# A hybrid decoder layer on one core: the input norm in fixed turns on each engine, idle products of another kind, and the keys' products tied

## The chip, the core and the metric

The kernel runs on one core of a Trainium2 chip. The time is device microseconds of one execution. Engines are called as in the profile: PE (TensorE, matrix products; PEld is its weight load), ACT (ScalarE), DVE (VectorE), POOL (GpSimd) and SP (SyncE, which here only issues transfers). Each engine works through its own list of instructions in order and waits on semaphores for what other engines or transfers deliver.

## What is computed

512 tokens of 1024 values go through one layer. The input is normed once, and everything else starts from the normed input `h`: the mLSTM branch, the sliding-window attention with its queries, keys and values, and two gates. The output projection, an MLP, a gated embedding and a last norm follow.

```python
def rmsnorm(x, g):
    xf = x.astype(jnp.float32)
    xf = xf * lax.rsqrt(jnp.mean(xf * xf, axis=-1, keepdims=True) + EPS)
    return xf.astype(x.dtype) * g.astype(x.dtype)
...
        h = rmsnorm(x, norm_mix_g[i])
        proj = h @ w_in[i]
        qk_ml, v_ml, o_ml, if_pre, q_sw, k_sw, v_sw, g_a, g_b = jnp.split(proj, split_idx, axis=-1)
```

The change concerns the norm, the product that gives `v_sw` (256 columns) and `if_pre` (8 columns), and where the product that gives `k_sw` may stand.

## The kernel before

Every float32 product is done as three products of two parts: an operand is split into a high part, a copy in the type fp32r, and a low part, the difference. `split` does the first on ACT and the second on DVE; `pairs` lists the three products (high with high, high with low, low with high), and `chain` issues them (L171). A product's last operand is thus always a low part.

The start works on four tiles of 128 tokens (`NT` = 4), in this order:

- SP loads the norm's weight (`grow`, one row of 1024), then x tile by tile (`xt`, the first in two halves) and the three pieces (`K3`: 3, 3 and 2 of the 8 blocks of 128 rows) of the weight of the values and gates (`w_vsif`, raw pieces `wv`, split into `wh` and `wl` by `load_vs_w`, the high part on POOL, L327, the low part on DVE, L328).
- The weight's row is split into parts (`gparts`) and spread over 128 partitions by four products with a row of ones, into `gmix` (L275). Between them PE does idle products of a matrix of ones (`stir`, L263): 5 before, 1 in the middle, 3 behind.
- `norm(m)`: ACT squares the tile and sums (L296), ACT takes the root (L283), DVE the reciprocal (L285), and DVE scales the tile by it and by `gmix` in two halves (L300).
- `columns(m, xn)`: PE transposes the eight blocks (L311, into two banks for even tiles, `pst`, and one wide one for odd tiles, `psa`), ACT copies the high part into `h` (L316), DVE makes the low part (L317), and ACT keeps an unsplit copy `hf` for tiles 1 to 3 (L321).
- The values' product of a tile is 24 products of 264 columns (`mm_tok`), 9, 9 and 6 by the weight's pieces; ACT copies out the values (`vs`, L352) and DVE adds the gates' bias (L353).
- Then come the keys, two groups of 24 products of 512 columns (`proj_T(w_ksw, i, ps_t)`), the first queries (`q_proj(0)`) and the mLSTM's values (`by_tokens`).

A scheduler sets the order of instructions within an engine from their order in the program, their readiness and the places given by `tc.issue_after` (what is inside comes behind the named instruction) and `tc.keep_in_program_order` (the instruction keeps its place among those of its engine). Before, only the idle products and the weight's four products are kept in order. A tile of memory comes from a pool with a few buffers under one tag; an instruction that takes a buffer over waits for those that used it. The raw weights (`wr`) have four, their parts (`wh`, `wl`) four each, the banks `pst`, `psg`, `psa` two each, the scratch of tokens (`lm`, which holds `grow`, the scaled tiles `xn` and later four of the mLSTM value weight's eight pieces `wq`) four.

Of the kernel before, what the change touches and what calls it, by code (L numbers as in the profile page):

```python
# [36 lines left out]
def block_kernel(  # L37
# [49 lines left out]
    def nm(s):  # L87
        n_names[0] += 1
        return f"{s}_{n_names[0]}"


    def ps_g():
        return pp.tile([P, 512], F32, tag="g", bufs=2, name=nm("psg"))

    def ps_t():
        return pp.tile([P, 512], F32, tag="t", bufs=2, name=nm("pst"))

    def ps_a():
        return pp.tile([P, 1024], F32, tag="a", bufs=2, name=nm("psa"))
# [34 lines left out]
    def split(dst, src, scale=None):  # L134

        if scale is None:
            A.copy(dst[0], src)  # L137
            last_low[0] = V.tensor_sub(dst[1], src, r32(dst[0]))  # L138
# [26 lines left out]
        return [(a[0], b[0]), (a[0], b[1]), (a[1], b[0])]  # L165

    last_mm = [None]

    def chain(ps, ops, first, last, parts=False):
        for i, (l, r) in enumerate(ops):  # L170
            last_mm[0] = T.matmul(ps, l, r, start=first and i == 0, stop=last and i == len(ops) - 1, skip_group_check=parts)  # L171

    def quads(src, tags):

# [17 lines left out]
    def mm_tok(ps, w, acts, m, first=True, last=True):  # L192
# [4 lines left out]
        chain(ps, ops, first, last)  # L197

    nc.scalar.preload_act_table_set("sqrt_and_others")


    ident = cp.tile([P, P], F32, name="ident")
# [29 lines left out]
            o = slice(c * D // n, (c + 1) * D // n)  # L232
            nc.sync.dma_start(out=xt[m][:, o], in_=x[m * P : (m + 1) * P, o])

    grow = tok_scratch("grow")[:1, :]
    nc.sync.dma_start(out=grow, in_=g_mix)
    load_x(0, 2)

    K3 = [slice(0, 3), slice(3, 6), slice(6, 8)]
# [18 lines left out]

    idle = [ps_g(), ps_g()]

    def stir(n, bank=0):
        for i in range(n):
            tc.keep_in_program_order(T.matmul(idle[bank][:, :P], ones, ones, start=True, stop=True))  # L263

    one_row = c1.tile([1, P], F32R, name="one_row")
    A.copy(one_row, ones[:1, :])
    gmix = ps_a()
    gparts = [[act_r("gm")[:1, :] for _ in range(2)] for _ in range(2)]
    for c in range(2):
        split(gparts[c], grow[:, c * 512 : (c + 1) * 512])  # L270
    stir(5)
    for i in range(2):
        for c in range(2):
            tc.keep_in_program_order(
                T.matmul(gmix[:, c * 512 : (c + 1) * 512], one_row, gparts[c][i], start=i == 0, stop=i == 1, skip_group_check=True)  # L275
            )
        stir(1 if i == 0 else 3, i)

    def rstd_of(ss, n):

        w = ss.shape[1]
        sd = small("sd", w)
        A.activation(sd, ss, AF.Sqrt, bias=eps_t, scale=1.0 / n)  # L283
        rs = small("rs", w, 5)
        V.reciprocal(rs, sd)  # L285
        return rs
# [3 lines left out]
    h2, hT = big_hl("h")  # L290
    hf = [None]

    def norm(m):
        xn = tok_scratch("xn")
        ss = small("ss", 1)
        A.activation(xn, xt[m], AF.Square, accum_out=ss)  # L296
        rs = rstd_of(ss, D)
        for c in range(2):
            o = slice(c * 512, (c + 1) * 512)
            done = V.scalar_tensor_tensor(xn[:, o], xt[m][:, o], rs, gmix[:, o], ALU.mult, ALU.mult)  # L300
        return xn, done.ins

    def columns(m, xn):

        if m % 2:
            ps = ps_a()
            halves = [ps[:, :512], ps[:, 512:]]
        else:
            halves = [ps_t(), ps_t()]
        for k in range(KT):  # L310
            T.transpose(halves[k // 4][:, k % 4 * P : (k % 4 + 1) * P], xn[:, k * P : (k + 1) * P], ident)  # L311
        n = 8 if m % 2 else 4
        for k in range(0, KT, n):
            dst = [t[:, k : k + n, m * P : (m + 1) * P] for t in h2]
            src = (ps if m % 2 else halves[k // 4]).rearrange("p (k c) -> p k c", k=n)
            first = A.copy(dst[0], src)  # L316
            second = V.tensor_sub(dst[1], src, r32(dst[0]))  # L317
            if m:
                if k == 0:
                    hf.append(tk("hf")[:, :D].rearrange("p (k c) -> p k c", k=KT))  # L320
                A.copy(hf[m][:, k : k + n, :], src)  # L321
        return first.ins, second.ins

    def load_vs_w(c):
        n = K3[c].stop - K3[c].start
        hl = [wp.tile([P, 1024], F32R, tag=t, bufs=WB, name=nm(t))[:, : n * 264] for t in ("wh", "wl")]
        G.tensor_copy(hl[0], wv[c][:, : n * 264])  # L327
        V.tensor_sub(hl[1], wv[c][:, : n * 264], r32(hl[0]))  # L328
        return [q.rearrange("p (k c) -> p k c", k=n) for q in hl]

    xn, normed = norm(0)
    with tc.issue_after(normed):
        wv[0] = load_vs_w(0)
    on_scalar, _ = columns(0, xn)
    with tc.issue_after(on_scalar):
        xn, normed = norm(1)
    with tc.issue_after(normed):
        wv[1:] = [load_vs_w(1), load_vs_w(2)]
    _, on_vector = columns(1, xn)
    for m in range(NT):  # L340
        if m == 1:
            with tc.issue_after(on_vector):
                xn, _ = norm(2)
            columns(2, xn)
        elif m == 2:
            columns(3, norm(3)[0])

        ps = ps_g()
        for c in range(3):
            mm_tok(ps[:, :264], wv[c], hT[K3[c]], m, first=c == 0, last=c == 2)  # L350
        t = sp.tile([P, 256], F32, tag="vs", bufs=4, name=nm("vs"))
        A.copy(t, ps[:, :256])  # L352
        gate_in = V.tensor_add(gt[:, m, :], ps[:, 256:264], bif)  # L353
# [8 lines left out]


    hf[0] = tk("hf")[:, :D].rearrange("p (k c) -> p k c", k=KT)
    with tc.issue_after(gate_in.ins):
        hi, lo = [r32(t[:, :, :P]) for t in h2]
        V.tensor_add(hf[0], hi, lo)

# [33 lines left out]
    HALF = [slice(0, 64), slice(64, 128)]  # L402
    kk, kl = [], []
    for i in range(2):
        ps = proj_T(w_ksw, i, ps_t)
        both = [act_r("kk"), act_r("kk")]
        low = [act_r("kl"), act_r("kl")]
        for ab in range(2):
            s, o = HALF[ab], HALF[1 - ab]
            A.copy(both[ab][s, :], ps[s, :])  # L410
            V.tensor_sub(low[ab][s, :], ps[s, :], r32(both[ab][s, :]))
            nc.sync.dma_start(out=r32(both[ab])[o, :], in_=r32(both[ab])[s, :])
            nc.sync.dma_start(out=r32(low[ab])[o, :], in_=r32(low[ab])[s, :])
        kk.append(both)
        kl.append(low)
# [12 lines left out]
    q_proj(0)  # L428

    S3, S4 = [], []  # L430

# [92 lines left out]

    pg = ps_a()
    pgi, pgf = pg[:, :512], pg[:, 512:]
    for m in range(NT):
        T.transpose(pgi[:4, m * P : (m + 1) * P], gt[:, m, :4], ident)
        T.transpose(pgf[:4, m * P : (m + 1) * P], gt[:, m, 4:], ident)
    by_tokens(w_vml, post_by_tokens(put_v), True)  # L530


    def row(n):
# [220 lines left out]
    V.tensor_scalar_mul(nsink, sink, -1.0)  # L754


    vd = [None] + [sp.tile([P, 256], F32, tag="vd", bufs=2, name=nm("vd")) for _ in range(2)] + [vs[3]]
    for n in (3, 2, 1):
        V.tensor_sub(vd[n], vs[n], vs[n - 1])
# [671 lines left out]
```

## Time and profile before

| | |
|---|---|
| Time, median of 3 runs | 882.57 us (881.98 to 882.72) |
| The profiled execution | 882.08 us, span 880.3 us |
| PE busy | 868.6 us, 99% of the span |
| DVE, ACT, POOL busy | 662.1, 481.8, 28.9 us |
| PE busy in 0 to 22 us | 19.80 us |
| PE busy in 22 to 100 us | 78.00 us |
| Granted TensorE clock | 0.999 |

A row of the timeline reads: start, duration, engine, line, operation, output <- inputs, partitions x elements, and how many instructions are merged into the row; in brackets the idle time of the engine before it and what ended it. Starts are counted from the span's start. Durations of products are modelled and overlap, so the distance between starts is the time that one takes from the next. A row of stretches gives: the stretch, its length, then the busy time of PE, PEld, DVE, ACT and POOL with their numbers of instructions, the granted clock, the share of the transfer engines and GB/s.

### The profile page before, as it was taken

Reading aid. Unit: us, or ns where it says so; the run is one execution under the profiler, and the core shown is the slowest. Engines: PE = TensorE matmul, PEld = TensorE weight load, DVE = VectorE, ACT = ScalarE, POOL = GpSimd, SP = SyncE. Lnnn points to the kernel's source line nnn. Section 1 sums busy time; section 2 is a strip of 40 time slices with the busy share of each in tenths; the row PEclk is TensorE's granted clock in tenths of the full one; section 3 lists DMA queues with packets and bytes.
Section 4 is the critical chain, followed back from the end, with each engine's and each line's share of the span. In section 5 each row is a group of like instructions: output and inputs, shape, how many; then the busy total and the mean of one; then the engine's idle time right before and its main releaser. Section 6 shows DMA issues by size and latency. Waiting matters only on the chain.

```text
span 880.3 us, 11620 instructions
## 1 busy us (share of the span) xinstructions
PE 868.6 (99%) x4404; PEld 727.8 (83%) x4404; DVE 662.1 (75%) x980; ACT 481.8 (55%) x808; POOL 28.9 (3%) x52
## 2 busy tenths in 40 slices
PE   8999999999999999999999999999999999999996
PEld 7888889998777777888888888888888888878886
DVE  6999888875789876666896669657956884689566
ACT  6684554544775768743344665356335534544843
POOL 1111010000000000000020000000000000000000
PEclk9999999999999999999999999999999999999999
DMA  7765244436122162364244612620452064101402
GB/s 266 211 180 184 73 156 163 170 110 193 49 73 72 49 211 75 100 241 139 72 90 149 220 44 77 210 96 1 140 171 72 1 195 140 48 25 54 163 1 95
DMA packets 32361, 105.16 MB, mean 119 GB/s; under 512 B 4525, under 2 KB 5037, under 8 KB 32306
## 3 DMA queue, kind: packets, MB, share of 16 engines
q1 hardware_dynamic: 28002, 93.15, 32.0%
q0 software_dynamic: 4160, 11.02, 4.8%
q8 instruction: 34, 0.56, 0.3%
q10 hardware_dynamic: 144, 0.26, 0.1%
q14 instruction: 21, 0.17, 0.1%
HBM read 91.30 MB, written 8.40 MB: 113 GB/s over the span
## 4 chain that ended last, share of the span: by engine, by line
PE 75%; DVE 3%; ACT 3%; issue 1%; DMA 0%; SPq 0%; ACTq 0%
PE psg L171 43%; PE psp L171 22%; PE psa L171 4%; PE psa L831 1%; PE pst L747 1%; DVE wl L138 1%; ACT lm L712 1%; PE psa L819 1%; ACT wh L137 1%; PE psa L689 1%; PE psa L690 1%; PE psa L726 0%; PE pst L873 0%; PE psp L988 0%; DVE qs L425 0%
## 5 line engine op out<-in xcount | busy, mean ns | idle before, releaser
L137 ACT CAST wh<-wr 128x1024 fp32r<-128x1024 f32 x138 | 144.8, 1051 | 179.0 <-PE psg L171 74.8
L138 DVE TENSOR_TENSOR wl<-wr,wh 128x1024 fp32r<-128x1024 f32 x138 | 167.5, 1219 | 83.6 <-ACT wh L137 82.5
L171 PE MATMUL psg<-x,wh 128*128 128x512 f32 x512 | 157.7, 389 | 0.0
L171 PE MATMUL psp<-wh,uf 128*128 128x512 f32 x448 | 139.2, 390 | 0.0
L171 PEld LDWEIGHTS psg<-x,wh 128*128 128x128 f32 x512 | 96.0, 188 | 19.8
L171 PE MATMUL psg<-x,wl 128*128 128x512 f32 x256 | 99.6, 389 | 0.0
L171 PEld LDWEIGHTS psp<-wh,uf 128*128 128x128 f32 x448 | 84.1, 188 | 17.4
L171 PE MATMUL psp<-wl,uf 128*128 128x512 f32 x224 | 87.2, 390 | 0.0
L171 PE MATMUL psg<-h,wh 128*128 128x512 f32 x256 | 81.0, 395 | 0.6 <-DVE rc L715 0.6
L137 ACT CAST wh<-wd 128x1024 fp32r<-128x1024 f32 x44 | 46.2, 1052 | 57.0 <-PE psp L171 23.0
L138 DVE TENSOR_TENSOR wl<-wd,wh 128x1024 fp32r<-128x1024 f32 x44 | 53.2, 1219 | 16.0 <-ACT wh L137 15.9
L171 PEld LDWEIGHTS psg<-x,wl 128*128 128x128 f32 x256 | 48.0, 188 | 10.1
L171 PEld LDWEIGHTS psg<-h,wh 128*128 128x128 f32 x256 | 47.0, 188 | 11.2 <-issue 1.6
L171 PE MATMUL psg<-h,wl 128*128 128x512 f32 x128 | 50.5, 395 | 0.0
L138 DVE TENSOR_TENSOR uf<-F,uf 128x1792 fp32r<-128x1792 f32 (+2 forms) x20 | 33.0, 1652 | 21.8 <-ACT uf L137 21.8
L171 PEld LDWEIGHTS psp<-wl,uf 128*128 128x128 f32 x224 | 42.0, 188 | 8.7
L171 PE MATMUL psg<-yb,wh 128*128 128x512 f32 x128 | 41.3, 402 | 0.1
L171 PE MATMUL psg<-ya,wh 128*128 128x512 f32 x128 | 39.5, 390 | 0.0
L137 ACT CAST uf<-F 128x1792 fp32r<-128x1792 f32 (+2 forms) x20 | 27.9, 1396 | 20.5 <-DVE F L1133 20.4
L1157 DVE SCALAR_TENSOR_TENSOR xk<-psp,r,xk 128x512 f32<-128x512 f32 x48 | 33.8, 745 | 3.5 <-PE psp L171 3.2
L171 PE MATMUL psg<-hS,wh 128*128 128x256 f32 x192 | 35.6, 284 | 0.0
L171 PE MATMUL psa<-h,wh 128*128 128x256 f32 x192 | 35.3, 285 | 0.3 <-ACT p L625 0.2
(323 smaller groups left out, 1753.5 us busy)
## 6 DMA issues: line engine op xcount, KB each, us to landing
wr<-in_w_up SPq DMA_DIRECT2D x32, 512.0 KB, 3.3
wd<-in_w_down SPq DMA_DIRECT2D x24, 512.0 KB, 3.6
wr<-in_w_qsw SPq DMA_DIRECT2D x8, 512.0 KB, 4.2
gd<-gr POOLq DMA_DIRECT2D x8, 512.0 KB, 3.6
wr<-in_w_qkml SPq DMA_DIRECT2D x8, 512.0 KB, 3.3
wr<-in_w_b SPq DMA_DIRECT2D x8, 512.0 KB, 3.3
gl<-gd SPq DMA_DIRECT2D x8, 512.0 KB, 3.3
wr<-in_w_a SPq DMA_DIRECT2D x8, 512.0 KB, 4.5
```

Of the source, the lines that this page charges most:

```text
L137: A.copy(dst[0], src)
L138: last_low[0] = V.tensor_sub(dst[1], src, r32(dst[0]))
L171: last_mm[0] = T.matmul(ps, l, r, start=first and i == 0, stop=last and i == len(ops) - 1, skip_group_check=parts)
L689: T.matmul(o, q[:, n * P : (n + 1) * P], kk[kp][ab][:, k0 : k0 + 256], start=True, stop=False)
L690: T.matmul(o, q[:, n * P : (n + 1) * P], kl[kp][ab][:, k0 : k0 + 256], start=False, stop=True)
L712: A.activation(lm3[:, g, :], lm3[:, g, :], AF.Exp, bias=nmx[:, g : g + 1], scale=0.125, accum_out=sm[:, g : g + 1])
L747: T.matmul(o[HALF[ab], :], v[:, c : c + 64], w[:, ab * 512 : (ab + 1) * 512], start=j == 0, stop=j == len(terms) - 1)
L819: T.matmul(psc, qk[4 + h][:, n0 : n0 + P], qk[h][:, n0:], start=True, stop=True, skip_group_check=True)
L831: last_mm[0] = T.matmul(pn[:, t % 2, : DV + 1], wT[s][:, t * P : (t + 1) * P], vm[s][:, h, :], start=s == 0, stop=s == t, skip_group_check ...
L1157: pin(V.scalar_tensor_tensor(o, ps[:, t, :], r2[:, 2 * toks + t : 2 * toks + t + 1], o, ALU.mult, ALU.add))
```

## The change

The start is written out again, with nearly every instruction up to the first two products of tile 3 kept in the order of the program, and with other idle products.

- `grow` is loaded from ACT's queue, as the first instruction of ACT, so x is the first load of SP.
- The idle products take `varied`, a 128x512 tile that POOL fills with an integer pattern (`iota`) and DVE converts. There are four, of 512 columns each, all ahead of the weight's four products.
- The row's two high parts are made on ACT and DVE, one each, and `one_row` on DVE.
- Tile 0 is squared in halves (the first half's sum becomes the bias of the root) and scaled in quarters.
- The high parts of the values' weight are made on ACT, not on POOL.
- `square`, `scale`, `turn`, `high`, `low`, `whole`, `high_w`, `low_w`, `product` and `finish_vs` are then called in a written order. Tiles 2 and 3 are transposed in two halves each, between the products of the tile before.
- The keys' weight may be cast only behind `whole(1, 2)` on ACT and the last scale on DVE, and the keys' products stand behind the last product issued. Differences of values (`vd`), `nsink`, the gates' transposes and the loads and products of `by_tokens` get places of their own.

```diff
+    pin = tc.keep_in_program_order
...
             last_mm[0] = T.matmul(ps, l, r, start=first and i == 0, stop=last and i == len(ops) - 1, skip_group_check=parts)
+            if pinned:
+                pin(last_mm[0])
...
+    grow = tok_scratch("grow")[:1, :]
+    nc.scalar.dma_start(out=grow, in_=g_mix)
     nc.scalar.preload_act_table_set("sqrt_and_others")
+    steps = act_f("steps").bitcast(mybir.dt.int32)
+    G.iota(steps, pattern=[[5, 512]], base=1, channel_multiplier=3)
...
-    grow = tok_scratch("grow")[:1, :]
-    nc.sync.dma_start(out=grow, in_=g_mix)
...
-    def stir(n, bank=0):
+    varied = act_r("varied")
+    one_row = c1.tile([1, P], F32R, name="one_row")
+    pin(V.tensor_copy(one_row, ones[:1, :]))
+    pin(V.tensor_copy(varied, steps))
+
+    def stir(n, bank):
         for i in range(n):
-            tc.keep_in_program_order(T.matmul(idle[bank][:, :P], ones, ones, start=True, stop=True))
-
-    one_row = c1.tile([1, P], F32R, name="one_row")
-    A.copy(one_row, ones[:1, :])
+            pin(T.matmul(idle[bank], varied[:, :P], varied, start=True, stop=True))
+
...
+    pin(A.copy(gparts[0][0], grow[:, :512]))
+    pin(V.tensor_copy(gparts[1][0], grow[:, 512:]))
     for c in range(2):
-        split(gparts[c], grow[:, c * 512 : (c + 1) * 512])
-    stir(5)
+        pin(V.tensor_sub(gparts[c][1], grow[:, c * 512 : (c + 1) * 512], r32(gparts[c][0])))
+    stir(3, 0)
+    stir(1, 1)
...
+    def square(m, n=1):
...
+            pin(A.activation(xn[m][:, o], xt[m][:, o], AF.Square, accum_out=ss))
+            if c < n - 1:
+                part = small("bias", 1, 1)
+                pin(V.tensor_scalar(part, ss, 1.0 / D, EPS, ALU.mult, ALU.add))
+                bias = part
+        sd = small("sd", 1)
+        pin(A.activation(sd, ss, AF.Sqrt, bias=bias, scale=1.0 / D))
+        return sd
...
+    def high_w(c):
+        pin(A.copy(wvp[c][0], wv[c][:, : wvp[c][0].shape[1]]))
+
+    def low_w(c):
+        pin(V.tensor_sub(wvp[c][1], wv[c][:, : wvp[c][0].shape[1]], r32(wvp[c][0])))
...
+    sd = square(0, 2)
+    scale(0, sd, (0, 1, 2, 3), 4)
+    high_w(0)
+    turn(0, 0)
+    turn(0, 1)
+    high(0, 0)
+    high(0, 1)
+    low_w(0)
+    low(0, 0)
+    low(0, 1)
+    product(0, 0)
+    sd = square(1)
+    scale(1, sd, (0, 1), 2)
+    high_w(1)
+    high_w(2)
+    turn(1, 0)
+    turn(1, 1)
+    low_w(1)
+    low_w(2)
+    product(0, 1)
+    product(0, 2)
+    high(1, 2)
+    sd = square(2)
+    low(1, 2)
+    scale(2, sd, (0, 1), 2)
+    sd = square(3)
+    finish_vs(0)
+    product(1, 0)
+    turn(2, 0)
+    product(1, 1)
+    turn(2, 1)
+    high(2, 0)
+    high(2, 1)
+    scale(3, sd, (0,), 2)
+    low(2, 0)
+    low(2, 1)
+    on_vector = scale(3, sd, (1,), 2)
+    on_scalar = whole(1, 2)
+    product(1, 2)
+    finish_vs(1)
+    product(2, 0)
+    turn(3, 0)
+    product(2, 1)
+    turn(3, 1)
+    product(2, 2)
+    whole(2, 0)
+    whole(2, 1)
+    high(3, 2)
+    low(3, 2)
+    finish_vs(2)
+    whole(3, 2)
+    for c in range(3):
+        product(3, c)
+    finish_vs(3)
...
-        ps = proj_T(w_ksw, i, ps_t)
+        with tc.issue_after(on_vector), tc.issue_after(on_scalar):
+            w = load_w(w_ksw[i], KT * P, KT)
+        ps = ps_t()
+        with tc.issue_after(last_mm[0].ins):
+            mm_T(ps, w, hT)
```

How instructions move is seen best in the lists of the engines. First PE's list from the program's start to tile 0's first product, before and then after. `psg_131` and `psg_132` (after: 133 and 134) are the banks of the idle products, `psa_135` (139) is `gmix`, `pst` are the banks of tile 0's transposes.

```order
1 L263 MATMUL psg_131<-ones 128x128 x5
2 L275 MATMUL psa_135<-gm_136,one_row 128x512
3 L275 MATMUL psa_135<-gm_138,one_row 128x512
4 L263 MATMUL psg_131<-ones 128x128
5 L275 MATMUL psa_135<-gm_137,one_row 128x512
6 L275 MATMUL psa_135<-gm_139,one_row 128x512
7 L263 MATMUL psg_132<-ones 128x128 x3
8 L311 MATMUL pst_173<-ident,xn_160 128x128 x4
9 L311 MATMUL pst_174<-ident,xn_160 128x128 x4
```

```order
1 L273 MATMUL psg_133<-varied_135 128x512 x3
2 L273 MATMUL psg_134<-varied_135 128x512
3 L285 MATMUL psa_139<-gm_140,one_row 128x512
4 L285 MATMUL psa_139<-gm_142,one_row 128x512
5 L285 MATMUL psa_139<-gm_141,one_row 128x512
6 L285 MATMUL psa_139<-gm_143,one_row 128x512
7 L338 MATMUL pst_181<-ident,xn_165 128x128 x4
8 L338 MATMUL pst_182<-ident,xn_165 128x128 x4
```

No idle product stands between the weight's products and tile 0's transposes any more.

Second, PE's list around tile 3's transposes. `psg_271` is the bank of tile 1's values' product, `psg_321` that of tile 2 (after: `psg_310`), `psg_354` that of tile 3; `psa_308` (after: `psa_320`) is the bank of tile 3's transposes; `h_158` and `h_159` (after: `h_157` and `h_158`) are the high and low parts of the normed input.

```order
58 L171 MATMUL psg_271<-wh_200,h_158 128x264
59 L171 MATMUL psg_271<-wl_201,h_158 128x264
60 L171 MATMUL psg_271<-wh_200,h_159 128x264
61 L311 MATMUL psa_308<-ident,xn_299 128x128 x8
62 L171 MATMUL psg_321<-wh_169,h_158 128x264
63 L171 MATMUL psg_321<-wl_170,h_158 128x264
```

```order
78 L172 MATMUL psg_310<-wh_161,h_158 128x264
79 L338 MATMUL psa_320<-ident,xn_254 128x128 x4
80 L172 MATMUL psg_310<-wh_163,h_157 128x264
81 L172 MATMUL psg_310<-wl_164,h_157 128x264
82 L172 MATMUL psg_310<-wh_163,h_158 128x264
83 L172 MATMUL psg_310<-wh_163,h_157 128x264
84 L172 MATMUL psg_310<-wl_164,h_157 128x264
85 L172 MATMUL psg_310<-wh_163,h_158 128x264
86 L172 MATMUL psg_354<-wh_159,h_157 128x264
87 L172 MATMUL psg_354<-wl_160,h_157 128x264
88 L172 MATMUL psg_354<-wh_159,h_158 128x264
```

Before, all eight transposes of tile 3 stand ahead of the 24 products of tile 2. Now the last four stand ahead of the last six of them, and the ninth product behind them is the first that reads tile 3's low part.

Third, ACT's list around tile 3's high part (`psa_308`, after `psa_320`). `wh_410` (after `wh_414`) is the high part of the keys' first weight, `hf` the unsplit copies, `vs` the values.

```order
16 L352 COPY vs_242<-psg_217 128x256
17 L321 COPY hf_215<-psa_204 128x1024
18 L316 CAST h_158<-pst_254 128x4x128
19 L137 CAST wh_410<-wr_408 128x1024
20 L321 COPY hf_266<-pst_254 128x512
21 L316 CAST h_158<-pst_255 128x4x128
22 L352 COPY vs_296<-psg_271 128x256
23 L316 CAST h_158<-psa_308 128x8x128
```

```order
19 L380 COPY vs_259<-psg_196 128x256
20 L348 CAST h_157<-pst_272 128x4x128
21 L348 CAST h_157<-pst_273 128x4x128
22 L358 COPY hf_299<-psa_217 128x1024
23 L380 COPY vs_307<-psg_262 128x256
24 L358 COPY hf_344<-pst_272 128x512
25 L358 COPY hf_344<-pst_273 128x512
26 L137 CAST wh_414<-wr_412 128x1024
27 L348 CAST h_157<-psa_320 128x8x128
```

The keys' weight now stands directly ahead of tile 3's high part, and both casts of tile 2 stand ahead of the unsplit copies.

More of the change, by code (lines that the diff above doesn't have):

```diff
@@ L167, in block_kernel, with chain @@
     last_mm = [None]
-    def chain(ps, ops, first, last, parts=False):
+    pin = tc.keep_in_program_order
+    def chain(ps, ops, first, last, parts=False, pinned=False):
         for i, (l, r) in enumerate(ops):
             last_mm[0] = T.matmul(ps, l, r, start=first and i == 0, stop=last and i == len(ops) - 1, skip_group_check=parts)
+            if pinned:
+                pin(last_mm[0])
     def quads(src, tags):
@@ L190, in mm_T, with mm_tok @@
         chain(ps, ops, first, last)
-    def mm_tok(ps, w, acts, m, first=True, last=True):
+    def mm_tok(ps, w, acts, m, first=True, last=True, pinned=False):
         ops = []
@@ L291, in block_kernel @@
     hf = [None]
[L293 to L350, printed above, removed]
-        t = sp.tile([P, 256], F32, tag="vs", bufs=4, name=nm("vs"))
-        A.copy(t, ps[:, :256])
-        gate_in = V.tensor_add(gt[:, m, :], ps[:, 256:264], bif)
-        vs.append(t)
+    xn, turned = [None] * NT, [None] * NT
@@ new lines, in square @@
+    def square(m, n=1):
+        xn[m] = tok_scratch("xn")
+        bias = eps_t
+        for c in range(n):
+            o = slice(c * D // n, (c + 1) * D // n)
+            ss = small("ss", 1)
+            pin(A.activation(xn[m][:, o], xt[m][:, o], AF.Square, accum_out=ss))
[6 more added lines that the diff above has]
+        return sd
@@ new lines, in scale, with turn @@
+    def scale(m, sd, parts, n):
+        if parts[0] == 0:
+            rstd[m] = small("rs", 1, 5)
+            pin(V.reciprocal(rstd[m], sd))
+        for c in parts:
+            o = slice(c * D // n, (c + 1) * D // n)
+            done = pin(V.scalar_tensor_tensor(xn[m][:, o], xt[m][:, o], rstd[m], gmix[:, o], ALU.mult, ALU.mult))
+        return done.ins
+    rstd = [None] * NT
+    def turn(m, c):
+        if c == 0:
+            if m % 2:
+                t = ps_a()
+                turned[m] = [t[:, :512], t[:, 512:], t]
+            else:
+                turned[m] = [ps_t(), ps_t()]
+        for k in range(4 * c, 4 * c + 4):
+            pin(T.transpose(turned[m][c][:, k % 4 * P : (k % 4 + 1) * P], xn[m][:, k * P : (k + 1) * P], ident))
@@ new lines, in columns_in, with high, low, whole @@
+    def columns_in(m, c):
+        k = slice(4 * c, 4 * c + 4) if c < 2 else slice(0, KT)
+        dst = [t[:, k, m * P : (m + 1) * P] for t in h2]
+        return k, dst, turned[m][c].rearrange("p (k c) -> p k c", k=k.stop - k.start)
+    def high(m, c):
+        _, dst, src = columns_in(m, c)
+        pin(A.copy(dst[0], src))
+    def low(m, c):
+        _, dst, src = columns_in(m, c)
+        return pin(V.tensor_sub(dst[1], src, r32(dst[0]))).ins
+    def whole(m, c):
+        k, _, src = columns_in(m, c)
+        if c != 1:
+            hf.append(tk("hf")[:, :D].rearrange("p (k c) -> p k c", k=KT))
+        return pin(A.copy(hf[m][:, k, :], src)).ins
@@ new lines, in block_kernel, with product @@
+    wvp = [[wp.tile([P, 1024], F32R, tag=t, bufs=WB, name=nm(t))[:, : (q.stop - q.start) * 264] for t in ("wh", "wl")] for q in K3]
+    def high_w(c):
+        pin(A.copy(wvp[c][0], wv[c][:, : wvp[c][0].shape[1]]))
+    def low_w(c):
+        pin(V.tensor_sub(wvp[c][1], wv[c][:, : wvp[c][0].shape[1]], r32(wvp[c][0])))
+    vs_ps = [None] * NT
+    def product(m, c):
+        if c == 0:
+            vs_ps[m] = ps_g()
+        w = [q.rearrange("p (k c) -> p k c", c=264) for q in wvp[c]]
+        mm_tok(vs_ps[m][:, :264], w, hT[K3[c]], m, first=c == 0, last=c == 2, pinned=True)
@@ L526, in block_kernel @@
     pgi, pgf = pg[:, :512], pg[:, 512:]
[L527 to L530, printed above, removed]
+    with tc.issue_after(last_mm[0].ins):
+        for m in range(NT):
+            T.transpose(pgi[:4, m * P : (m + 1) * P], gt[:, m, :4], ident)
+            T.transpose(pgf[:4, m * P : (m + 1) * P], gt[:, m, 4:], ident)
+    with tc.issue_after(normed):
+        by_tokens(w_vml, post_by_tokens(put_v), True)
     def row(n):
```

25 lines of the change are left out of this document (16 added, 9 removed).

## The prediction

> **What bounds the kernel now.** I read the page first, then the busy time of each engine by stretches, then the timeline of the first 45 us in order of time. The page says how little TensorE (PE) idles in the whole span, and the three stretches say where: in each row the second number is PE's busy time.
>
> ```profile
> span 880.3 us, 11620 instructions
> PE 868.6 (99%) x4404; PEld 727.8 (83%) x4404; DVE 662.1 (75%) x980; ACT 481.8 (55%) x808; POOL 28.9 (3%) x52
> 0.00:22.00 22.00, 19.80 (x110) 16.87 (x111) 14.97 (x28) 14.93 (x27) 3.73 (x13) 1.00 0.79 266
> 22.00:44.00 22.00, 22.00 (x122) 18.92 (x121) 20.18 (x28) 14.65 (x23) 3.55 (x4) 1.00 0.77 211
> 44.00:100.00 56.00, 56.00 (x258) 46.08 (x257) 53.46 (x70) 36.12 (x45) 7.82 (x15) 1.00 0.54 162
> ```
>
> From 22 to 100 us PE is never idle. The change ends before that, so its worth is one number: when the first product of the keys starts. A shift there passes to the end one for one. Of the first 22 us, the first tile carries the wait:
>
> ```profile
> 0.73 1.28 ACT L199 ACT_TABLE_LOAD   x1 [0.73 <-PEq L1419]
> 0.74 0.36 SPq L236 DMA_DIRECT2D grow<-in_g_mix  x1
> 1.15 0.83 SPq L233 DMA_DIRECT2D xt<-in_x  x2
> 4.80 1.06 ACT L296 ACTIVATE xn<-xt 128x1024 f32<-128x1024 f32 x1 [1.41 <-DMA xt<-in_x]
> 5.36 1.22 PE L275 MATMUL psa<-gm,one_row 1*128 1x512 f32 x2
> 6.30 0.16 DVE L285 RECIPROCAL rs<-sd 128x1 f32<-128x1 f32 x1 [2.12 <-ACT sd L283]
> 6.50 1.65 PE L263 MATMUL psg<-ones 128*128 128x128 f32 x6
> 6.61 1.41 DVE L300 SCALAR_TENSOR_TENSOR xn<-xt,rs,psa 128x512 f32<-128x512 f32 x2
> 6.93 0.84 POOL L327 CAST wh<-wr 128x792 fp32r<-128x792 f32 x1 [5.14 <-DMA wr<-in_w_vsif]
> 7.95 1.91 PE L311 MATMUL pst<-ident,xn 128*128 128x128 f32 x8
> 9.04 0.58 ACT L316 CAST h<-pst 128x512 fp32r<-128x512 f32 x1 [2.77 <-PE pst L311]
> 9.90 0.58 ACT L316 CAST h<-pst 128x512 fp32r<-128x512 f32 x1 [0.27 <-PE pst L311]
> 10.38 1.07 ACT L296 ACTIVATE xn<-xt 128x1024 f32<-128x1024 f32 x1
> ```
>
> Scaling starts at 6.61, right behind the spreading of the weight (5.36 + 1.22 = 6.58) and of the reciprocal (6.46). The transposes could start when its first half is done, but PE is in idle products until 8.1, so they end at 9.86. From there a chain leads through tile 1 to the keys:
>
> ```profile
> 11.57 0.29 ACT L283 ACTIVATE sd<-ss,eps_t 128x1 f32<-128x1 f32 x1
> 14.25 1.01 ACT L316 CAST h<-psa 128x1024 fp32r<-128x1024 f32 x1 [1.02 <-PE psa L311]
> 15.29 1.23 DVE L317 TENSOR_TENSOR h<-psa,h 128x1024 fp32r<-128x1024 f32 x1 [0.28 <-ACT h L316]
> 16.57 0.51 PE L171 MATMUL psg<-wh,h 128*128 128x264 f32 x2
> 20.25 1.03 PE L311 MATMUL psa<-ident,xn 128*128 128x128 f32 x8
> 21.32 1.02 ACT L316 CAST h<-psa 128x1024 fp32r<-128x1024 f32 x1 [0.24 <-PE psa L311]
> 22.60 1.21 DVE L317 TENSOR_TENSOR h<-psa,h 128x1024 fp32r<-128x1024 f32 x1
> 26.93 0.62 PE L171 MATMUL pst<-h,wh 128*128 128x512 f32 x2
> ```
>
> Tile 1's low part ends at 16.52 and the product that needs it starts at 16.57. From there PE works without a break to the keys at 26.93: 10.36 us for 70 products and 16 transposes. Tile 3's transposes end at 21.28, ahead of all of tile 2's products, which hide its high part (21.32) and low part (to 23.81).
>
> **Part by part, up to tile 0.** SP loses one issue, so x starts 0.41 earlier (1.15 - 0.74) and is whole at 4.80 - 0.41 = 4.39. The Square now runs in halves, the first under the second's transfer; the second takes about 0.6 (a 128x512 row of ACT has 0.58). From the end of the Square (5.86) to that of the reciprocal (6.46) are 0.60, so scaling could start at 5.65. The weight's row goes to ACT's queue ahead of the table load (0.73 to 2.01); that may push ACT by one issue, 0.36, which is idle time before x.
>
> The spread weight must be ready too. Its products stand behind four wide ones, which wait for an iota on POOL and a copy of it on DVE. Neither is in this trace; the nearest rows are these.
>
> ```profile
> 1.11 0.29 POOL masks.py:199 TENSOR_SCALAR_AFFINE_SELECT ident<-ident 128x128 f32<-128x128 f32 x1
> 2.90 1.28 DVE L138 TENSOR_TENSOR gm<-grow,gm 1x512 fp32r<-1x512 f32 x2 [1.90 <-ACT gm L137]
> ```
>
> 128 columns of a pattern cost POOL 0.29, so 512 cost between 0.29 and 1.16; I take 0.8, nearer the upper end since it is four times the columns. From 0.73 that is 1.5, and with 0.6 for the copy (two of 512 columns take 1.28) PE starts at 2.15. Two products of 512 columns took 1.22, 0.43 apart. Eight of them end at 2.2 + 7 x 0.43 + 0.79 = 6.0; so scaling starts at 6.0 with a slow clock, at 5.65 with a fast one.
>
> The clock is what I know least. The granted clock reads 1.00 from the start, yet products of one shape have two speeds:
>
> ```profile
> 9.77 0.56 PE L171 MATMUL psg<-wh,h 128*128 128x264 f32 x1
> 11.01 0.42 PE L171 MATMUL psg<-wl,h 128*128 128x264 f32 x1
> 11.23 0.47 PE L171 MATMUL psg<-wh,h 128*128 128x264 f32 x2
> 11.54 0.28 PE L171 MATMUL psg<-wl,h 128*128 128x264 f32 x1
> 11.67 0.41 PE L171 MATMUL psg<-wh,h 128*128 128x264 f32 x2
> ```
>
> They are 0.22 apart until 11.2 and 0.13 after 11.5, though PE has been occupied since 1.05. The Trainium skill (TensorE: Matmul & The Clock Gate, Part 1) says that the clock opens after a window of about 3.4 us of sustained activity, and Part 4 that transposes don't count as activity in the same way. The trace agrees that the ten narrow products and the transposes did not open it. By that rule the 3.4 us of wide and weight products would open it by about 5.6, and the sum would be the fast one of the two below.
>
> Quarters of the scale (1.41 / 4 = 0.35) feed two transposes each, with no idle products between. Slow: the first pair starts at 6.45, eight at 0.21 end near 8.35. Fast: DVE paces and they end near 7.6. Before, 9.86. The weight's high part moves from POOL (0.84) to ACT, ahead of tile 0's: its data come at 6.93 - 0.41 = 6.5, done at 7.4, no later than the transposes it stands before; if its data are not earlier, the fast case loses 0.4. Tile 1's Square starts behind tile 0's second cast, at 10.38 before, now at 8.9 slow or 8.1 fast.
>
> **Tile 1.** Square to end of low part was 10.38 to 16.52, 6.14. ACT gets two more weight casts there, about 0.85 + 0.63, in the gap between 11.86 (the root's end) and 14.25. So the low part ends at 15.0 slow, 14.25 fast: 1.5 to 2.25 gained.
>
> **Tiles 2 and 3 give it back.** Tile 3's transposes are now in two parts among tile 2's products, the last six products behind them. Tile 3's third product needs its low part. From the transposes' end: cast 1.02, low 1.21, three handoffs of 0.04, 2.35 in all. PE has six products of tile 2 and two of tile 3, 8 x 0.13 = 1.04, begun some 0.15 before the transposes' modelled end: it idles 2.35 + 0.15 - 1.04 = 1.5. Before, 24 products stood there. Small waits of transposes for scales add 0.1. Keys start at 15.05 + 10.36 + 1.6 = 27.0 slow, 14.3 + 11.96 = 26.3 fast, against 26.93: +0.1 or -0.6.
>
> **What is moved and hidden.**
>
> ```profile
> 18.79 1.06 ACT L137 CAST wh<-wr 128x1024 fp32r<-128x1024 f32 x1
> 20.79 1.22 DVE L138 TENSOR_TENSOR wl<-wr,wh 128x1024 fp32r<-128x1024 f32 x1
> 22.03 0.33 SPq L181 DMA_DIRECT2D wr<-in_w_vml  x1
> 25.24 0.75 DVE L759 TENSOR_TENSOR vd<-vs,vs 128x256 f32<-128x256 f32 x2
> 32.42 1.05 ACT L137 CAST wh<-wr 128x1024 fp32r<-128x1024 f32 x1 [3.69 <-issue]
> 56.05 1.23 DVE L138 TENSOR_TENSOR wl<-wr,wh 128x1024 fp32r<-128x1024 f32 x1 [0.93 <-ACT wh L137]
> wr<-in_w_vml SPq DMA_DIRECT2D x4, 512.0 KB, 3.7
> ```
>
> The keys' weight (1.06 on ACT, 1.22 on DVE) now stands just ahead of tile 3's casts on both; by then tile 3's transposes are barely done, so it costs 0 to 0.1. On SP a value weight's load (22.03) now queues behind one that waits for tile 3's transposes; issued near 23.6 and landing 3.7 later, it is 5 us ahead of its cast at 32.42. The differences (0.75) move to DVE's later queue, which still has 0.93 idle at 56. The tie of the keys' products changes no order on PE: they stood behind tile 3's already.
>
> **The sum** is made against the profiled execution, 882.08 (span 880.3), 0.49 below the median 882.57. Between +0.1 and -0.6 I take -0.3, a clock that opens while tile 0 is turned: four wide products are 1.7 us of dense work, more than the 1.3 us from the first product (9.77 to 11.1) that preceded the opening before, but a stop follows them. 881.8 on that execution's scale, **882.3** against the median.
>
> **The rivals.** *The pattern is late (slower).* If POOL's iota takes longer than my bound, PE's first eight products, the scale and all behind them move with it, since the weight's spread is already the last to arrive. With 2.5 us instead of 0.8 the keys start at 28.7, +1.8; with 3, +2.2: 884.8. It decides above 0.8 and makes it slower by over 0.2% from 2.5 us on. For it: no such instruction in the trace; against: POOL's rows here, 0.29 and 0.84, are under 1 us. 0.13.
>
> *The clock opens late.* Work up to 12 us now has more holes (waits for low parts and for tile 1's scale), so the opening could slip to 15. Then the last 15 products of tile 0 (from about 12.8, 15 x 0.22 = 3.3) end near 16.1, past the 15.0 of tile 1's low part, and hold up tile 1: +1.0 on the slow case, 883.7. For it: it took 10 us before. 0.14.
>
> *No gap before tile 3's products (faster).* If its parts come sooner than I chain them, the fast start is kept whole: -0.6 - 1.5 = -2.1, 880.5. Against it: the rows of cast and low part leave no room. 0.13. That the order isn't what the edit says can be left out: each engine's instructions are listed in the section on the change.
>
> **How the numbers follow.** The forecast has 0.60. A difference of 0.2%, 1.8 us, is about what can be told from none. Faster by more: the third rival, 0.13. Slower: the first and a tail of the second, 0.16. Within: 0.71. The range goes from 881.0, beyond the fast end by the 0.7 that the runs scatter, to 884.2, past the late clock and part of the late pattern.
>
> **What would show it.** Steps right: scaling of tile 0 from 5.6 to 6.0; its last transpose by 7.6 to 8.4; tile 1's low part done by 14.2 to 15.0; PE idle 1.5 us, released by DVE's low part, before tile 3's third product; keys between 26.3 and 27.0; nothing idle from there to 100 us. Wrong: keys before 25.2 or after 28.7, an iota of over 2 us, products 0.22 apart after 13 us, or new idle time of PE behind the keys.

## The result and the profile after

The changed kernel takes 883.06 us (median of 22 runs, 882.08 to 884.70), the kernel before in the same rounds 882.04 (median of 22, 881.47 to 882.72): a ratio of 1.0013, interval 1.0007 to 1.0019. The forecast was 0.3 us faster and no difference that can be told; it is 1.0 us slower, and the interval does not reach down to a ratio of 1. The time lies inside the range that was given, but on the other side of the kernel before. The profiled execution took 883.07, span 881.3, against 882.08 and 880.3.

First the page and the three stretches of the kernel after (per stretch: its length, then the busy time of PE, PEld, DVE, ACT and POOL).

```profile
span 881.3 us, 11601 instructions
PE 867.8 (98%) x4390; PEld 726.7 (82%) x4390; DVE 664.0 (75%) x986; ACT 483.8 (55%) x811; POOL 27.6 (3%) x50
0.00:22.00 22.00, 18.77 (x98) 15.95 (x99) 16.20 (x34) 15.38 (x29) 2.52 (x11) 1.00 0.86 308
22.00:44.00 22.00, 20.84 (x110) 17.73 (x109) 18.62 (x24) 14.95 (x23) 3.55 (x4) 1.00 0.60 152
44.00:100.00 56.00, 56.00 (x261) 45.90 (x261) 54.08 (x72) 37.08 (x46) 7.80 (x15) 1.00 0.53 160
```

Before, PE had no idle time from 22 to 44 us; now it has 1.16 there (22.00 - 20.84), and none from 44 to 100. The timeline of the kernel after, up to tile 1's transposes:

```profile
0.84 0.56 POOL L206 IOTA steps<- 128x512 int32 x1 [0.39 <-POOLq L1514]
1.95 2.08 PE L273 MATMUL psg<-varied 128*128 128x512 f32 x4 [1.95 <-DVE varied L269]
3.96 2.07 PE L285 MATMUL psa<-gm,one_row 1*128 1x512 f32 x4
6.06 1.66 DVE L325 SCALAR_TENSOR_TENSOR xn<-xt,rs,psa 128x256 f32<-128x256 f32 x4 [0.16 <-PE psa L285]
6.69 1.94 PE L338 MATMUL pst<-ident,xn 128*128 128x128 f32 x8 [0.67 <-DVE xn L325]
9.14 1.06 ACT L310 ACTIVATE xn<-xt 128x1024 f32<-128x1024 f32 x1
11.75 1.94 PE L338 MATMUL psa<-ident,xn 128*128 128x128 f32 x8 [0.58 <-DVE xn L325]
14.37 0.42 PE L172 MATMUL psg<-wl,h 128*128 128x264 f32 x1
14.77 1.22 DVE L352 TENSOR_TENSOR h<-psa,h 128x1024 fp32r<-128x1024 f32 x1 [1.00 <-ACT h L348]
14.99 0.28 PE L172 MATMUL psg<-wl,h 128*128 128x264 f32 x1
16.19 0.41 PE L172 MATMUL psg<-wh,h 128*128 128x264 f32 x2
```

Tile 0 is ahead of before as planned: its last transpose ends at 8.63 instead of 9.86, and tile 1's Square starts at 9.14 instead of 10.38. But tile 1's transposes, whose modelled time for eight was 1.22 before, take 1.94, and products stay 0.22 apart until 14.9 (before, 11.2). So of 1.24 us gained at the Square only 0.53 is left at the end of tile 1's low part (15.99 against 16.52), and 0.38 at the product that needs it, tile 1's third (16.19 against 16.57). Then the same timeline around tile 3:

```profile
22.59 0.60 PE L338 MATMUL psa<-ident,xn 128*128 128x128 f32 x4
23.23 1.01 ACT L348 CAST h<-psa 128x1024 fp32r<-128x1024 f32 x1
24.30 0.39 PE L172 MATMUL psg<-wh,h 128*128 128x264 f32 x1 [0.38 <-ACT h L348]
24.31 1.22 DVE L352 TENSOR_TENSOR h<-psa,h 128x1024 fp32r<-128x1024 f32 x1
25.58 0.51 PE L172 MATMUL psg<-wh,h 128*128 128x264 f32 x2 [0.78 <-DVE h L352]
28.35 0.63 PE L172 MATMUL pst<-h,wh 128*128 128x512 f32 x2
```

PE waits 0.38 for tile 3's high part and 0.78 for its low part: the gap. The keys start at 28.35 against 26.93, 1.42 later, while the span is 1.0 longer. Most of the difference between the two is a wait for a transfer that before's execution had and this one did not:

```profile
783.61 0.44 PE L1207 MATMUL psg<-ident,ptok 128*128 128x128 f32 x2 [0.51 <-DMA ptok<-in_p]
```

### The profile page after: what moved, and what is told of

Same layout as the page of the kernel before. It is cut to its first block, busy times and chain, and to the rows that moved or that the text cites. A ratio compares the mean times of both kernels' runs of the same rounds, so it can differ in the third digit from the quotient of the medians.

```text
span 881.3 us, 11601 instructions
## 1 busy us (share of the span) xinstructions
PE 867.8 (98%) x4390; PEld 726.7 (82%) x4390; DVE 664.0 (75%) x986; ACT 483.8 (55%) x811; POOL 27.6 (3%) x50
## 4 chain that ended last, share of the span: by engine, by line
PE 89%; DVE 5%; ACT 4%; issue 1%; DMA 1%; SPq 0%; ACTq 0%; DVEq 0%
PE psg L172 49%; PE psp L172 22%; PE psa L172 7%; PE pst L172 4%; PE psa L926 1%; PE pst L840 1%; DVE wl L138 1%; ACT wh L137 1%; ACT lm L805 1%; PE psa L914 1%; PE psa L782 1%; PE psa L783 1%; DMA wr<-in_w_gb 0%; PE psp L1075 0%; PE psa L819 0%
## 5 line engine op out<-in xcount | busy, mean ns | idle before, releaser
L172 PEld LDWEIGHTS psg<-h,wh 128*128 128x128 f32 x256 | 47.0, 188 | 11.2 <-issue 1.6
```

## The experiments

My theory after the result: the gap ahead of tile 3's third product costs a little over 1 us, and the front, which should have paid for it, gained almost nothing because the clock opened late ("the clock opens" is short for the moment at which products of one shape change from 0.22 to 0.13 us apart). The rivals: the wide idle products are to blame for the late opening; the holes between PE's works are; the keys' tie, or the keys' weight ahead of tile 3's parts, costs something. All ran in five rounds beside the kernel before, whose median was 882.01, 882.07 and 882.12 in the three sets; keys and products are read from one profiled execution each.

**Tile 3's transposes undivided, ahead of tile 2's products.**

```diff
     finish_vs(0)
+    on_scalar = whole(1, 2)
     product(1, 0)
...
     scale(3, sd, (0,), 2)
+    on_vector = scale(3, sd, (1,), 2)
     low(2, 0)
     low(2, 1)
-    on_vector = scale(3, sd, (1,), 2)
-    on_scalar = whole(1, 2)
     product(1, 2)
     finish_vs(1)
+    turn(3, 0)
+    turn(3, 1)
     product(2, 0)
-    turn(3, 0)
     product(2, 1)
-    turn(3, 1)
     product(2, 2)
```

The second half of tile 3's scale and tile 1's unsplit copy move forward with them.

> The changed kernel with tile 3's transposes undivided and ahead of all of tile 2's products, as before the change (its second half of the scale and tile 1's unsplit copy move forward so that neither is waited for). Theory one (the lost time is the slow clock up to 14.9 us plus the gap ahead of tile 3's products): the 1.2 us of idle PE in front of tile 3 go, the keys start 1.1 us sooner, 881.9 us, no slower than the kernel before. Theory two (the slow clock alone; the gap only takes the place of another wait): a new wait of about 1 us appears in tile 2's products and the time stays within 0.3 us of the changed kernel's 883.1.

Measured: 881.90 us, ratio 0.9994 (0.9985 to 1.0003). The gap is gone and the keys start at 26.93, though here the clock opened later still, with the last product of 0.42 at 15.69:

```profile
15.69 0.42 PE L172 MATMUL psg<-wl,h 128*128 128x264 f32 x1
21.82 1.02 ACT L348 CAST h<-psa 128x1024 fp32r<-128x1024 f32 x1
22.87 1.22 DVE L352 TENSOR_TENSOR h<-psa,h 128x1024 fp32r<-128x1024 f32 x1 [0.36 <-ACT h L348]
26.93 0.63 PE L172 MATMUL pst<-h,wh 128*128 128x512 f32 x2
```

The low part now ends at 24.09 under the 24 products of tile 2. So the place of tile 3's transposes costs 1.16 us in the median and 1.42 at the keys: the whole loss.

**Narrow idle products instead of wide ones.**

```diff
-            pin(T.matmul(idle[bank], varied[:, :P], varied, start=True, stop=True))
+            pin(T.matmul(idle[bank][:, :P], ones, ones, start=True, stop=True))
...
-    stir(3, 0)
+    stir(4, 0)
```

> The changed kernel with the idle products of before in front: five narrow ones of the matrix of ones instead of four wide varied ones, nothing else moved. If the kind of idle product matters to the clock, the products stay 0.22 us apart for longer than until 14.9, and the time is 0.5 us or more above the changed kernel's. If it doesn't matter (the clock goes by how unbroken PE's work is, and opens in tile 1's transposes and products either way), the time is within 0.3 us of it, 882.8 to 883.4.

**Two wide idle products in each of the two holes** (behind the weight's products and behind tile 0's first piece).

```diff
             pin(T.matmul(gmix[:, c * 512 : (c + 1) * 512], one_row, gparts[c][i], start=i == 0, stop=i == 1, skip_group_check=True))
+    stir(2, 1)
...
     product(0, 0)
+    stir(2, 1)
     sd = square(1)
```

> The changed kernel with four more wide idle products where PE waits: two between the weight's products and tile 0's transposes, two between tile 0's first products and tile 1's transposes. Theory one (the clock opens when PE's work has been unbroken for some 3.4 us; the holes at 6.0 and 11.0 keep it shut): products are 0.12 apart from 11.3 us or sooner, tile 1's transposes take 1.2 instead of 1.9, the keys start 1 us sooner, 882.0. Theory two (the moment of opening is chance, not the holes): opening stays between 11 and 15 and the time is 883.1 to 883.3.

Measured: 883.46 (ratio 1.0016, 1.0007 to 1.0025) and 883.74 (1.0016, 1.0007 to 1.0024). In both executions the clock opened near 11, as before. Nothing here speaks for the wide products as the cause of a late opening: with narrow ones it came early, but so it did with wide ones in a run told below (tile 3 in halves, 10.87). With the holes filled, the opening and the transposes came as in theory one, but the time did not. From each, the narrow kernel first:

```profile
9.34 1.06 ACT L310 ACTIVATE xn<-xt 128x1024 f32<-128x1024 f32 x1
11.95 1.22 PE L338 MATMUL psa<-ident,xn 128*128 128x128 f32 x8 [0.44 <-DVE xn L325]
14.26 1.22 DVE L352 TENSOR_TENSOR h<-psa,h 128x1024 fp32r<-128x1024 f32 x1 [0.29 <-ACT h L348]
27.83 0.63 PE L172 MATMUL pst<-h,wh 128*128 128x512 f32 x2
```

```profile
5.95 1.22 PE L273 MATMUL psg<-varied 128*128 128x512 f32 x2
12.00 1.22 PE L339 MATMUL psa<-ident,xn 128*128 128x128 f32 x8
27.86 0.62 PE L172 MATMUL pst<-h,wh 128*128 128x512 f32 x2
```

The keys came only 0.5 sooner than in the kernel after, and still 0.9 later than before. So a clock that opens 3.5 us earlier is worth 0.5 us here, not the 1.0 that my second rival had given it, and the gap is there with either. The medians did not improve even by that. Both profiled executions also lost about 1 us in waits near 181 and 190 us, told below; whether the other runs did is not on record.

**Both: undivided transposes and filled holes** (the first and the third edit together).

> Both of the first and the third together: holes filled and tile 3's transposes ahead of tile 2's products. If both causes are right their gains add, keys at 26.1 us, 880.9 us, 0.1% faster than the kernel before. If only the gap counts, 881.9; if only the clock, 882.0.

Measured: 881.67, ratio 0.9999 (0.9990 to 1.0008), not 880.9. From 1.95 us to the keys PE is idle for 0.32 us in all, and the keys start at 26.45, 0.48 sooner than before, not 0.8. In the time nothing is left of that that can be told from none. Tile 1's third product started at 15.59, 0.98 sooner than before, so half of the gain is lost again behind it. Part of that is the next chain, tile 3's low part, which ends at 23.63, just ahead of the product that needs it:

```profile
22.41 1.22 DVE L353 TENSOR_TENSOR h<-psa,h 128x1024 fp32r<-128x1024 f32 x1 [0.37 <-ACT h L349]
23.69 0.51 PE L172 MATMUL psg<-wh,h 128*128 128x264 f32 x2
```

Before, the low part ended at 23.81 and that product started at 24.27.

**The keys' products untied** (their weight keeps its place).

```diff
-        with tc.issue_after(last_mm[0].ins):
-            mm_T(ps, w, hT)
+        mm_T(ps, w, hT)
```

> The kernel after, with the keys' products no longer tied behind the last product issued; their weight keeps its place. In the lists one keys' product of 512 columns then stands ahead of tile 3's third product, and one DVE difference of values moves back. My prediction said that the tie changes no order on PE and costs nothing. If the gap ahead of tile 3's third product can be filled so, PE does about 0.2 us of keys' work in it: the keys' second product and all behind it come 0.2 earlier, 882.9. The rival, that the tie matters for more than this one product (its first product takes the bank from others or pulls a weight's load), gives another order behind 30 us and 0.5 us or more either way.

Measured: 883.36, ratio 1.0016 (1.0008 to 1.0025), not 882.9. One keys' product does move into the gap and the second wait is 0.55 instead of 0.78:

```profile
24.62 0.40 PE L172 MATMUL pst<-h,wh 128*128 128x512 f32 x1
25.57 0.52 PE L172 MATMUL psg<-wh,h 128*128 128x264 f32 x2 [0.55 <-DVE h L352]
```

The 0.23 is there in the trace and not in the median, whose interval holds it. That the tie orders nothing, as I had written, is wrong by one product; that it costs nothing that can be seen in the time stands.

**No idle products at all**, with tile 3's transposes undivided.

```diff
-    stir(3, 0)
-    stir(1, 1)
```

> The kernel of e1_tile3_whole (tile 3's transposes undivided, ahead of tile 2's products) without any idle products. If idle products do nothing for the clock, it opens where it did there, near 16.2, and the keys start where they did, at 26.9 or 0.3 earlier as the weight's row is spread sooner: 881.6 to 881.9. If they count towards its opening, leaving them out makes it open about 2 us later, near 18, and the products up to there 0.22 instead of 0.13 apart: keys near 27.7, 882.7.

Measured: 881.57, ratio 0.9995 (0.9986 to 1.0004), keys at 26.41. The clock opened while tile 1's transposes ran:

```profile
3.27 2.11 PE L283 MATMUL psa<-gm,one_row 1*128 1x512 f32 x4 [3.27 <-ACT gm L277]
11.54 1.63 PE L336 MATMUL psa<-ident,xn 128*128 128x128 f32 x8 [0.26 <-DVE xn L323]
13.13 0.29 PE L172 MATMUL psg<-wl,h 128*128 128x264 f32 x1
```

That is earlier than with the four wide products in the kernel after. So the clock opens without any idle product.

**Tile 1's chain shorter** (on the kernel with both edits): the high parts of the weight's second and third pieces on POOL, the second's low part ahead of tile 1's scale, three of its products ahead of tile 1's transposes, tile 1's parts in halves.

```diff
-        pin(A.copy(wvp[c][0], wv[c][:, : wvp[c][0].shape[1]]))
+        pin((G.tensor_copy if c else A.copy)(wvp[c][0], wv[c][:, : wvp[c][0].shape[1]]))
...
     product(0, 0)
-    stir(2, 1)
     sd = square(1)
+    high_w(1)
+    high_w(2)
+    low_w(1)
     scale(1, sd, (0, 1), 2)
-    high_w(1)
-    high_w(2)
+    product(0, 1, slice(0, 1))
     turn(1, 0)
     turn(1, 1)
...
-    high(1, 2)
+    high(1, 0)
+    high(1, 1)
...
```

> The kernel of e4_both with tile 1's chain made shorter: the second and third pieces of the values' weight get their high parts on POOL and the second its low part ahead of tile 1's scale, three products of it stand ahead of tile 1's transposes in place of two idle ones, and tile 1's high and low parts are made in halves. If tile 1's third product is held by that chain alone, it comes 0.5 to 0.6 sooner than 15.6 and the keys start at 25.9, 881.1. If PE's own work holds it as much, the keys stay at 26.3 to 26.5, 881.6.

Measured: 882.96, ratio 1.0010 (1.0001 to 1.0019), a miss. Tile 1's third product came at 15.31, 0.3 sooner than in the kernel with both edits, but a new wait ahead of tile 2's transposes took it back, and the keys started at 26.70:

```profile
15.31 0.51 PE L172 MATMUL psg<-wh,h 128*128 128x264 f32 x2 [0.20 <-DVE h L353]
17.04 0.63 PE L339 MATMUL pst<-ident,xn 128*128 128x128 f32 x4 [0.61 <-ACT xn L311]
```

That fits the profiled execution (881.92); why half of its runs lie above 882.9 is open.

**Tile 3's parts in halves**, all else as in the kernel after.

```diff
-    high(3, 2)
-    low(3, 2)
+    high(3, 0)
+    high(3, 1)
+    low(3, 0)
+    low(3, 1)
```

> The kernel after, with only tile 3's high and low parts made in halves. If the gap ahead of tile 3's third product is the chain of one whole high part and one whole low part (1.02 + 1.21), the first half's parts are ready early, as tile 3's first piece of the product reads only the first half's blocks: PE idles 0.3 us or less there, the keys start near 27.3, 882.0 to 882.2. If instead ACT and DVE are late there for other reasons (the keys' weight just ahead on both), the gap stays near 1 us and the time at 883.

**The same, with the keys' weight converted behind tile 3's parts.**

```diff
-    on_vector = scale(3, sd, (1,), 2)
-    on_scalar = whole(1, 2)
+    scale(3, sd, (1,), 2)
+    whole(1, 2)
...
-    high(3, 1)
+    on_scalar = high(3, 1)
...
-    low(3, 1)
+    on_vector = low(3, 1)
```

> The kernel of e8_tile3_halves with the keys' weight converted behind tile 3's parts on ACT and DVE instead of ahead of them. There PE still idled 0.71 us ahead of tile 3's third product, while DVE was in the keys' weight up to 24.06 though tile 3's first half was cast by 23.5. If that conversion is what is left of the gap, it goes: PE idles 0.2 us or less, the keys start near 26.8, 881.9. If the gap is the transposes' late place, it stays above 0.5 us.

Measured: 882.69 (ratio 1.0008, 1.0000 to 1.0017) and 882.74 (1.0007, 0.9998 to 1.0016). Halves left 0.71 of idle time, and so did the later weight, so the conversion of the keys' weight is not what holds the product. The rows of the second show what holds it:

```profile
22.79 0.60 PE L338 MATMUL psa<-ident,xn 128*128 128x128 f32 x4
23.42 1.07 ACT L348 CAST h<-psa 128x512 fp32r<-128x512 f32 x2 [1.02 <-PE psa L338]
24.53 1.29 DVE L352 TENSOR_TENSOR h<-psa,h 128x512 fp32r<-128x512 f32 x2 [2.25 <-ACT h L348]
25.28 0.51 PE L172 MATMUL psg<-wh,h 128*128 128x264 f32 x2 [0.71 <-DVE h L352]
```

ACT starts the first half only behind all eight transposes (23.42), and DVE the first low half only behind both high halves (23.42 + 1.07 = 24.49). The halves of this wide bank are released together in both kernels (why is not shown); only the last step, low half to product, is shortened. What is left of the gap goes with the transposes' late place, as the first experiment shows, and the keys' weight ahead of tile 3's parts costs nothing that shows.

**No idle products and tile 1's parts in halves**, tile 3 undivided.

> The kernel of e6_no_idle with tile 1's high and low parts in halves. There PE idled 0.29 us ahead of tile 1's third product, held by DVE's low part. With halves that wait goes and the keys start near 26.1, 881.3, if the clock opens by 13 as there; with an opening near 16 PE's own products hold that place and the keys start near 26.9, 881.9, as in e1_tile3_whole.

Measured: 881.23 (880.71 to 882.10), ratio 0.9991 (0.9982 to 1.0000), the lowest of all and 1.8 below the kernel after; against before it is at the edge of what can be told. In its profiled execution (881.78) the clock opened late (last 0.42 at 14.71), yet the keys came at 26.64, ahead of the 26.9 expected for that case.

**The kernel before without its nine idle products.**

```diff
-    stir(5)
...
-        stir(1 if i == 0 else 3, i)
```

> The kernel before without its nine idle products. If they do nothing for the clock, tile 0's transposes start when the first half of its scale is done, near 7.35 instead of 7.95, and end 0.7 sooner, the clock opens anywhere from 11 to 16, and the keys start between 26.1 and 27.0: 881.2 to 882.1. If they count, the clock opens later than in any run so far, behind 16.5, and the keys start at 27.5 or later, 882.7.

Measured: 882.48, ratio 1.0004 (0.9995 to 1.0013), no difference that can be told, though the time is 0.4 above what was expected; keys at 26.94 against 26.93. The clock opened within tile 1's transposes:

```profile
7.64 1.94 PE L309 MATMUL pst<-ident,xn 128*128 128x128 f32 x8 [2.58 <-DVE xn L298]
12.70 1.52 PE L309 MATMUL psa<-ident,xn 128*128 128x128 f32 x8 [0.45 <-ACT xn L294]
```

PE idled 2.58 us ahead of tile 0, and the keys lost nothing by it. Tile 0's transposes started 0.3 sooner than before, not 0.6.

## Why the prediction was wrong

**What stood.** The place to look (when the keys start; nothing idle from there to 100 us) was right. The iota took 0.56 (estimate 0.8, bounds 0.29 to 1.16), so the late pattern did not happen. Scaling started at 6.06 (5.65 to 6.0). The gap was predicted as 1.5 us of PE, released by DVE's low part; it is 1.16, in two waits, of which DVE's low part ends 0.78 and ACT's high part 0.38. From tile 1's third product to the keys I had 10.36 + 1.6 = 11.96; it is 28.35 - 16.19 = 12.16, so what tiles 2 and 3 give back was right to 0.2 us. The transfers behind the keys' weight, the differences of values and the weight itself cost nothing: PE is not idle from the keys to 100 us.

**What failed is the term for tile 1.** I had its low part done at 14.25 to 15.0, a gain of 1.5 to 2.25 that would pay for the gap; it ended at 15.99, a gain of 0.53. Three pieces add up. The Square started at 9.14, not 8.1 or 8.9: PE's clock did not open while tile 0 was turned, and the eight transposes ended at 8.63, 0.3 behind even the slow case. From the Square to the low part I took 6.14 us from before for both cases, but that stretch holds the eight transposes at 1.22, with the clock open; in the kernel after they took 1.94, and the stretch 6.85. In the narrow kernel, where they took 1.22, the stretch was 6.14 again (9.34 to 15.48). And the third product had to wait for PE's own products, 0.22 apart until 14.9, so it came at 16.19, 0.20 behind the low part. Added to the slow case's 15.05, the three (0.24, 0.71 and 0.20) give the measured place to 0.01 us. What is left of the gain, 0.38, does not pay for the 1.8 that tiles 2 and 3 give back.

**The clock opens late** was my rival with a chance of 0.14, from 11 to 15 us, and it is what the profiled execution shows (14.9). Its 883.7, 1.1 us above before, is near the measured 1.0 above, but its reasoning was only half right and the agreement is in part luck. It let PE's own products hold up tile 1 by 1 us, behind a low part that is done at 15.0; in the trace the low part itself came 1 us later, and the products added 0.20. And the runs with narrow products and with filled holes opened near 11 and still had their keys at 27.8 and no shorter times. With an open clock the front gains about 1.0 us at tile 1's third product, not 2. So the forecast was wrong in the open case too, because I counted the clock as open while tile 0 is transposed, where in all thirteen traces the eight take 1.91 to 1.94.

**When the clock opens** can't be read from how long PE has worked. In the kernel after, 4.1 us of unbroken products of 512 columns (1.95 to 6.03, the last four of them of one row) did not open it; with the holes filled, 5.2 us of them (1.95 to 7.17) did not either; and the earliest opening in any run was near 9.5. The Trainium skill (TensorE: Matmul & The Clock Gate, Part 1), which the prediction cites, says that about 3.4 us of sustained activity open it. These runs disagree with that. The same part of the Trainium skill says that the window runs freely and that the moment differs between runs of one kernel. With that the runs agree, as the last section shows.

**The tie** "changes no order on PE" was wrong by one product, without effect on the time. **The scale.** The profiled spans differ by 1.0 and the keys by 1.42; the 0.51 that before's execution lost at 783 us accounts for the difference within 0.1. The 0.49 that the sum added to get from the profiled execution to the median of 3 runs was chance: the median of 22 runs of the kernel before is 882.04, that of the profiled execution 882.08. The lower end of the range, as described there, is 882.57 - 0.6 - 0.7 = 881.3, not 881.0; nothing hangs on it.

## What to carry to other kernels

Look at what covers a conversion chain before an operation is split and its parts are set later: with the last four transposes behind 18 of the 24 products that had hidden a 2.3 us chain, the kernel lost 1.2 us, more than the rewritten front earned at the keys in any run. A duration taken from the trace of before belongs to the clock that it ran under; price a chain for both speeds before calling a gain. Idle products deserve a run without them: here no worth of either kind could be measured.

## What was not expected of the hardware

The moment at which products change from 0.22 to 0.13 apart differs between executions with the same work ahead of it, while the granted clock reads 1.00 throughout. The kernel after and those with tile 3 undivided, the keys untied and tile 3 in halves (two of these) have the same list of instructions on PE, ACT and DVE up to 14 us. Their last product of 0.42 started at 14.37, 15.69, 14.36, 10.87 and 15.10. The kernels with filled holes had theirs at 10.91, 10.91 and 9.09 (the third with only the first hole filled); those with no idle products at 10.86, 14.71 and 11.39; those with narrow ones at 11.01 (before) and 10.35. Filled holes and narrow products from 1 us on lie at the early end, with too few executions to call it a rule, and what sets the moment stays open.

Four of the thirteen profiled executions also lost 0.8 to 1.4 us of PE's time between 175 and 200 us, far behind the change. In that with tile 3 undivided (883.51, the longest of its 11 runs) a gate's weight landed late and PE waited twice, as it did in those with narrow products and filled holes:

```profile
176.76 1.22 DVE L539 TENSOR_TENSOR wq<-wr,wq 128x1024 f32<-128x1024 f32 x1 [1.96 <-DMA wr<-in_w_ga]
181.46 0.47 PE L172 MATMUL psa<-h,wh 128*128 128x256 f32 x2 [0.64 <-DVE t L712]
189.80 0.50 PE L172 MATMUL psa<-h,wh 128*128 128x256 f32 x2 [0.79 <-ACT p L718]
```

From the late weight on DVE works without a listed wait up to the instruction that releases PE at 181.46; the second wait was not traced back. In the kernel before DVE waited 0.31 for that weight and PE not at all there. Why it lands later in some executions was not found.
